# Mixing layers' weights split one layer ahead; a conv and a state space scan without GpSimd

## Chip, cores and metric

The kernel runs on one core of a Trainium2 chip. The metric is the device time of one execution in microseconds; the profile is one execution, taken by the hardware profiler. Engines: TensorE (PE; its weight loads are PEld), VectorE (DVE), ScalarE (ACT), GpSimd (POOL) and SyncE (SP), which issues every DMA.

## The reference, cut to what matters

Eight layers act on a residual stream of 512 tokens by 1024 channels: four of a first block (gated mixer a, windowed attention b, pooling mixer c, a again), then two sandwiches (mixer, feed-forward) of a second block. The change lies around the second block's mixers:

```python
def even_mixer(t, ...):                       # layer m0, the differential layer
    proj = t @ w_in
    y_a = diff_attention(proj[..., :1536])    # 4 heads, two softmaxes of width 64 each,
                                              # w = p0 - lam * p1, rmsnorm over the head
    y_b = conformer_conv(proj[..., 1536:])    # gate, causal conv of 31 taps, layernorm, silu
    return concatenate([y_a, y_b]) @ w_out

def odd_mixer(t, ...):                        # layer m1
    y_c = s5_ssm(u)       # b*u, complex scan over time with 1024 states, c*x, gelu, glu
    y_d = mla_attention(c_q, c_kv, k_r)       # 6 heads
    return concatenate([y_c, y_d]) @ w_out

def sandwich(x, g_pre, g_post, fn):
    return x + rmsnorm(fn(rmsnorm(x, g_pre)), g_post)
```

All in float32.

## The kernel before, in words

Activations lie channel by token, 128 channels to a tile of 512 tokens. A float32 product is made of three passes in fp32r: each operand is split into a high part (a copy rounded to fp32r) and a low part (the rest), and `mm3` adds high by high, high by low and low by high. For the activations `split` does it once; for the weights `wchunk` does it each time: `fetch` loads a chunk of up to 128 x 1024 into `wr`, ScalarE writes `wh`, VectorE (or GpSimd, in two halves) writes `wl = wr - wh`. Pool `pw` has three buffers of each of the three. `gemm_T` takes a chunk for one panel of 24 products, `gemm_tok` takes chunks of 24 products into four PSUM banks. After each chunk both call `tick`, which advances every generator in `tasks` by one step: that is how attention heads, the conv, the state space blocks and tables are placed among the projections. `drain` ticks until none is left. Pool `psg` has five PSUM banks for projections, head sums and turned softmaxes, `psa` three; pool `pt` has seven scratch tiles `t`.

The order in which the source issues instructions is a priority; a scheduler at build time lays out each engine's queue from it, so that work of a later step may stand earlier where an engine would be free. In `sandwich_end` TensorE and VectorE are pinned to source order.

`layer_c` (pooling, about 930 to 1285 us) runs two halves of 8 `c_wx` chunks, 8 `c_wz`, 8 half-size `c_wg` and 8 `c_wo`. `layer_m0` (from about 1643) opens with three of the eight `m0_wab` panels (conv value and gate), does the other five, then projects q and k of heads 0 and 1, all v, q and k of heads 2 and 3. `conv` does 23 of the 31 taps on VectorE (tile `cv`), eight as ScalarE products and GpSimd additions (tile `cvg`); `convs` runs the four convs, then the layer norm. Every third chunk of the q, k and v projections has its `wl` made by GpSimd (`share`). Then ticks run until all conv outputs are there, and `sandwich_end` starts with them (`k0=4`, `ahead`), projects out, adds to the residual and multiplies the first three panels of the next layer (weights `srcs`, two of them split by GpSimd). `layer_f` runs 22 gate and up panels and 24 down panels in three parts; in layer f0 the generator `ssm_tables` writes rotation tables (`srot`, `sbc`) to DRAM for m1. `layer_m1` projects, and `block` does one of eight groups of states: two fp32 products (`bu`), a rotation (`turn`: four products on VectorE, two additions on GpSimd), two scans, a rotation back, and `collect` multiplies by c on TensorE.

Of the kernel before, what the change touches and what calls it, by code (L numbers as in the profile page):

```python
# [40 lines left out]
def prepare(inp):  # L41
# [75 lines left out]
    A["m0_wo"] = _panels(np.concatenate([w[512:], w[:512]], axis=0))  # L117
# [62 lines left out]
def build(nc, tc, A, out, stages=("a0", "b", "c", "a1", "m0", "f0", "m1", "f1")):  # L180
# [40 lines left out]
    with ctx:  # L221
# [49 lines left out]
        share = [0, 0]  # L271

        def wchunk(src, n, eng=None):
# [3 lines left out]
            wr = early.pop(0) if early else fetch(src, n)  # L277
            wh = tl(pw, (P, 1024), "wh", F32R)
            wl = tl(pw, (P, 1024), "wl", F32R)
            S.activation(wh[:, :n], wr[:, :n], AF.Copy)  # L280
# [547 lines left out]
        def layer_c(nxt):  # L828
            with ExitStack() as c:
# [7 lines left out]
                for t in pads:  # L837
                    V.memset(t[:, 0:16], 0.0)
                npad = [0]
# [5 lines left out]
                for half in range(2):  # L845
                    Y = []
                    for g in (2 * half, 2 * half + 1):
# [25 lines left out]
                        for i in range(4):  # L873
                            ps = gemm_T(A["c_wg"][g, i], M)
                            V.scalar_tensor_tensor(Z[i], ps, csc[:, g * 4 + i:g * 4 + i + 1], Z[i],
                                                   op0=MUL, op1=MUL)
                            Y.append(split(py, "y", Z[i]))
                    for m in range(KD):
                        ps = gemm_T(A["c_wo"][half, m], Y)
                        V.tensor_tensor(xs[m], xs[m], ps, op=ADD)  # L880
                        if half:
                            finish_x(m)()

        def ffn_first(l):
            return [A[f"f{l}_w{n}"][i] for i in range(2) for n in "gu"] if f"f{l}" in stages else None

        def m1_first():
            return [A["m1_win"][i] for i in (2, 0, 1, 3)] if "m1" in stages else None


        def sandwich_end(W, Y, O, fresh, grow, srcs, pre=None, k0=0):
# [82 lines left out]
            if srcs:  # L974
                W1 = wchunk(srcs[1], D, G)
# [13 lines left out]
            W2 = wchunk(srcs[2], D, G)  # L989
# [55 lines left out]
        def layer_m0(nxt):  # L1045
            with ExitStack() as c:
# [3 lines left out]
                first, sc, sb = opening([A["m0_wab"][i] for i in range(3)], X)  # L1050
# [23 lines left out]
                def conv(i, up, y):  # L1074
                    def w(k):
                        return dw[:, i * 31 + k:i * 31 + k + 1]

                    def u(k):
                        return up[:, 2 + k:2 + k + NT]
                    nv = 31 - CONV_G  # L1080
                    g = tl(pm, (P, NT), "cvg")
                    for k in range(nv):
                        if k == 0:
                            V.tensor_scalar(y, u(0), w(0), cb[:, i:i + 1], op0=MUL, op1=ADD)
                            S.activation(g, u(nv), AF.Copy, scale=w(nv))
                        else:
                            V.scalar_tensor_tensor(y, u(k), w(k), y, op0=MUL, op1=ADD)
                        q = nv + 1 + k // 3
                        if k % 3 == 2 and q < 31:
                            t = tmp()  # L1090
                            S.activation(t, u(q), AF.Copy, scale=w(q))
                            G.tensor_tensor(g, g, t, op=ADD)
                        if k % 4 == 4 - 1:
                            yield
                    V.tensor_tensor(y, y, g, op=ADD)

                def convs():
# [11 lines left out]
                    ln = SumSq(4)  # L1109
# [5 lines left out]
                    rstd(r, ln.sums(), 1.0 / 512, 1e-5)  # L1115
                    lb = bcast(diagonal(r), pm, "cb")
                    yield
                    for i in range(4):
# [5 lines left out]
                        Y[i] = split(py, "y", C[i], 0.5)  # L1124
                        yield
                CV = []
                for i in range(4):
                    pu = first.pop(0) if first else gemm_T(A["m0_wab"][2 * i], X)
                    pb = first.pop(0) if first else gemm_T(A["m0_wab"][2 * i + 1], X)
# [10 lines left out]
                    if i == 0:  # L1140
                        tasks.append(convs())


                def project(a):

                    pss = gemm_tok([A["m0_wqk"][a, i] for i in range(4)], X, NT, 2)
# [27 lines left out]
                def attend(h, T):  # L1174
# [40 lines left out]
                    Y[4 + h] = split(py, "y", ps, sub)  # L1215
                share[:] = [3, 0]
                q = project(0)
                T = [flip_qk(q, 0), flip_qk(q, 1)]
                pss = gemm_tok([A["m0_wv"][i] for i in range(4)], X, NT, 2)
# [4 lines left out]
                tasks.append(attend(1, T[1]))  # L1224
                q = project(1)
# [3 lines left out]
                share[0] = 0  # L1229
                while any(Y[k] is None for k in range(4)):  # L1230
                    tick()
                sandwich_end(A["m0_wo"], Y, [tl(pa, (P, NT), "qkT") for _ in range(KD)], True, 8, ffn_first(0), k0=4)
# [134 lines left out]
        def layer_m1(nxt):  # L1367
            with ExitStack() as c:
# [34 lines left out]
                def block(j):  # L1403
# [12 lines left out]
                    def turn(a, b, minus):  # L1416

                        t1, t2, t3, t4 = tmp(), tmp(), tmp(), tmp()
                        V.tensor_tensor(t1, a, er, op=MUL)
                        V.tensor_tensor(t2, b, ei, op=MUL)  # L1420
                        G.tensor_tensor(t1, t1, t2, op=ADD if minus else SUB)  # L1421
                        V.tensor_tensor(t3, b, er, op=MUL)
                        V.tensor_tensor(t4, a, ei, op=MUL)
                        G.tensor_tensor(t3, t3, t4, op=SUB if minus else ADD)  # L1424
                        return t1, t3
                    yield
                    wr, wi = turn(bu[0], bu[1], True)
# [10 lines left out]
                    late.append((j, w, u, xr, xi))  # L1438

                def collect(j, w, u, xr, xi):  # L1440
# [3 lines left out]
                    PE.matmul(ya, lhsT=w[:, 2], rhs=xr, start=j % 4 == 0, stop=False)  # L1444
                    PE.matmul(ya, lhsT=w[:, 3], rhs=xi, start=False, stop=j % 4 == 3)
# [14 lines left out]
                def glu():  # L1460
# [4 lines left out]
                    wh, wl = wchunk(A["s_wg"], 512)  # L1465
# [27 lines left out]
                for i in range(2):  # L1493
                    ps = gemm_T(A["m1_win"][4 + i], X)
# [7 lines left out]
                wh, wl = wchunk(A["m1_wk"], 768)  # L1502
# [10 lines left out]
                wh, wl = wchunk(A["m1_wv"], 768)  # L1513
# [11 lines left out]
                for a in range(3):  # L1525
                    wh, wl = wchunk(A["m1_wq"][a], 1024)
# [53 lines left out]
                sandwich_end(A["m1_wo"], Y, O + [tl(pm, (P, NT), f"u{i}") for i in range(2)], True, 10, ffn_first(1))  # L1580


        def layer_f(l, nxt):
            with ExitStack() as c:
# [74 lines left out]
```

## Time and profile before

| | us |
|---|---|
| median of 3 runs | 2931.03 |
| lowest, highest | 2930.87, 2932.01 |
| the profiled execution | 2936.18 |
| its span, first to last instruction | 2933.7 |
| TensorE busy / VectorE / ScalarE / GpSimd | 2820.6 / 1642.2 / 1051.9 / 347.3 |
| mean granted clock of TensorE | 0.976 |

Times within the profile count from the first instruction. Matmuls are pipelined, so that a busy PE is not PE at its peak; the granted clock is 1.00 at 2.4 GHz and 0.5 at 1.2.

### The profile page before, as it was taken

The numbers are of one execution on the slowest core, as the hardware profiler recorded it, in microseconds if no ns is written. First come the engines' busy times: TensorE is split into PE (matmuls) and PEld (weight loads), VectorE is DVE, ScalarE is ACT, GpSimd is POOL, SyncE is SP. The second block draws the span as 40 slices with busy tenths as digits, with TensorE's granted clock in tenths as the row PEclk, the third lists the DMA queues.
The fourth block names the chain that finished last, engine by engine and source line by source line (L and its number), as shares of the span: only waits on it lengthen the run. The fifth ranks groups of instructions, "written<-read, shape, count | busy, mean of one in ns | idle before, by whom it ended". The sixth has DMA issues, their size and how long they took to land. (4 is left out here: it accounts for less than half of the span.)

```text
span 2933.7 us, 34524 instructions
## 1 busy us (share of the span) xinstructions
PE 2820.6 (96%) x13488; PEld 2331.9 (79%) x13488; DVE 1642.2 (56%) x3023; ACT 1051.9 (36%) x1679; POOL 347.3 (12%) x272
## 2 busy tenths in 40 slices
PE   8999999999999999999999987889999979999998
PEld 7888888888888888888888865678888845888886
DVE  4454654545556554544445697896443696543434
ACT  4322344444444322333223445442222435432222
POOL 2000000000000111210010252120000341300001
PEclk9999999999999999999999997889999999999999
DMA  4222332222223232322222211123332320132222
GB/s 161 94 86 94 129 111 87 87 80 94 72 94 95 94 101 89 120 93 94 93 94 92 90 63 44 48 96 136 111 105 92 113 90 22 58 101 100 94 99 67
DMA packets 87667, 270.08 MB, mean 92 GB/s; under 512 B 11728, under 2 KB 18640, under 8 KB 87504
## 3 DMA queue, kind: packets, MB, share of 16 engines
q1 hardware_dynamic: 87504, 267.88, 27.6%
q8 instruction: 105, 1.72, 0.2%
q14 instruction: 58, 0.48, 0.1%
HBM read 255.26 MB, written 12.58 MB: 91 GB/s over the span
## 5 line engine op out<-in xcount | busy, mean ns | idle before, releaser
L280 ACT ACTIVATE wh<-wr 128x1024 fp32r<-128x1024 f32 (+2 forms) x464 | 479.9, 1035 | 1329.8 <-PE g L205 1015.7
L205 DVE TENSOR_TENSOR wl<-wr,wh 128x1024 fp32r<-128x1024 f32 (+2 forms) x454 | 566.3, 1248 | 341.3 <-ACT wh L280 338.7
L205 PE MATMUL g<-xl,wh 128*128 128x512 f32 (+1 forms) x1720 | 661.6, 385 | 17.2 <-DVE xl L205 17.0
L205 PE MATMUL g<-xh,wh 128*128 128x512 f32 (+1 forms) x1720 | 663.7, 386 | 0.7 <-ACT wh L280 0.7
L205 PE MATMUL g<-xh,wl 128*128 128x512 f32 (+1 forms) x1720 | 658.1, 383 | 0.8 <-DVE wl L205 0.8
L205 PE MATMUL g<-wh,xh 128*128 128x512 f32 (+1 forms) x992 | 383.1, 386 | 16.9 <-ACT wh L280 8.9
L205 PE MATMUL g<-yh,wh 128*128 128x512 f32 (+1 forms) x1046 | 394.9, 378 | 1.4 <-DVE qr L205 1.4
L205 PE MATMUL g<-yh,wl 128*128 128x512 f32 (+1 forms) x1046 | 391.4, 374 | 3.1 <-DVE wl L205 3.1
L205 PEld LDWEIGHTS g<-xl,wh 128*128 128x128 f32 x1720 | 327.1, 190 | 83.0 <-DVE xl L205 22.9
L205 PE MATMUL g<-yl,wh 128*128 128x512 f32 (+1 forms) x1046 | 391.2, 374 | 0.0
L205 PE MATMUL g<-wl,xh 128*128 128x512 f32 (+1 forms) x992 | 377.8, 381 | 0.5 <-DVE wl L205 0.5
L205 PEld LDWEIGHTS g<-xh,wl 128*128 128x128 f32 x1720 | 327.3, 190 | 63.2 <-DVE wl L205 1.4
L205 PE MATMUL g<-wh,xl 128*128 128x512 f32 (+1 forms) x992 | 376.6, 380 | 0.0
L205 PEld LDWEIGHTS g<-xh,wh 128*128 128x128 f32 x1720 | 327.5, 190 | 61.2 <-ACT wh L280 1.2
L424 POOL TENSOR_TENSOR acc<-acc,t 128x256 f32<-128x256 f32 (+1 forms) x111 | 129.8, 1170 | 1654.5 <-issue 1406.4
L205 PEld LDWEIGHTS g<-wh,xh 128*128 128x128 f32 x992 | 188.5, 190 | 50.4 <-ACT wh L280 8.9
L205 PEld LDWEIGHTS g<-yh,wh 128*128 128x128 f32 x1046 | 198.4, 190 | 37.9 <-DVE qr L205 1.8
L205 PEld LDWEIGHTS g<-yh,wl 128*128 128x128 f32 x1046 | 198.1, 189 | 38.1 <-DVE wl L205 4.2
L205 PEld LDWEIGHTS g<-yl,wh 128*128 128x128 f32 x1046 | 198.3, 190 | 35.4 <-issue 1.2
L205 DVE TENSOR_TENSOR t<-g,sb 128x512 f32<-128x512 f32 x112 | 77.2, 690 | 251.4 <-PE g L205 251.4
L205 PEld LDWEIGHTS g<-wh,xl 128*128 128x128 f32 x992 | 188.4, 190 | 34.7 <-issue 0.2
L205 PEld LDWEIGHTS g<-wl,xh 128*128 128x128 f32 x992 | 188.6, 190 | 33.9 <-DVE wl L205 1.6
(315 smaller groups left out, 2728.5 us busy)
## 6 DMA issues: line engine op xcount, KB each, us to landing
wr<-in_f_wg_dram SPq DMA_DIRECT2D x44, 512.0 KB, 3.5
wr<-in_f_wu_dram SPq DMA_DIRECT2D x44, 512.0 KB, 3.5
wr<-in_a_wv_dram SPq DMA_DIRECT2D x32, 512.0 KB, 3.5
wr<-in_a_wu_dram SPq DMA_DIRECT2D x32, 512.0 KB, 3.4
wr<-in_a_wz_dram SPq DMA_DIRECT2D x32, 512.0 KB, 3.4
wr<-in_a_wo_dram SPq DMA_DIRECT2D x32, 512.0 KB, 3.5
wr<-in_b_wc_dram SPq DMA_DIRECT2D x32, 512.0 KB, 3.5
wr<-in_f_wd_dram SPq DMA_DIRECT2D x32, 512.0 KB, 3.5
```

The lines of the kernel that those rows point to most:

```text
L205: r = f(*a, **k)
L280: S.activation(wh[:, :n], wr[:, :n], AF.Copy)
L424: G.tensor_tensor(self.acc[:, t], self.acc[:, t], sq[:, t], op=ADD)
```

## The change

Weights of the two mixing layers, and the first four of the feed-forward layer behind each, are split one layer ahead: a generator `presplit` loads, splits and stores both parts to DRAM, for m0 while `layer_c` runs, for m1 while `layer_f(0)` runs. `wchunk` then loads `wh` and `wl` where it had loaded `wr` and split it. 32 weights (28 of m0, four of f0) and 24 (20 of m1, four of f1) are treated so. The differential layer's conv is all on VectorE, its sums of channels and of squares go to TensorE, two of its four conv inputs are projected later, and the rows of its output weight are reordered so that the closing projection starts with heads 0 and 1. In the state space blocks GpSimd's additions go to VectorE before the scans, and into TensorE's accumulation behind them.

```diff
 def prepare
-    A["m0_wo"] = _panels(np.concatenate([w[512:], w[:512]], axis=0))
+    A["m0_wo"] = _panels(np.concatenate([w[:256], w[512:], w[256:512]], axis=0))
...
+        def presplit(pool, todo):
+            made = []
+            def store():
+                w, wh, wl = made.pop(0)
+                nc.sync.dma_start(w.h, f32(wh))
+                nc.sync.dma_start(w.l, f32(wl))
+            for w in todo:
+                n = w.n
+                wr = tl(pool, (P, 1024), "pr")[:, :n]
+                wh, wl = (tl(pool, (P, 1024), "p" + a, F32R, bufs=2)[:, :n] for a in "hl")
+                nc.sync.dma_start(wr, w.src)
+                if made:
+                    store()
+                yield
+                S.activation(wh, wr, AF.Copy)
+                V.tensor_tensor(wl, wr, f32(wh), op=SUB)
+                made.append((w, wh, wl))
+            store()
 def wchunk
-            if eng is None:
-                share[1] += 1
-                eng = G if share[0] and share[1] % share[0] == 0 else V
+            if isinstance(src, Pre):
+                nc.sync.dma_start(f32(wh[:, :n]), src.h)
+                nc.sync.dma_start(f32(wl[:, :n]), src.l)
+                return wh, wl
...
-            step = n if eng is V else 512
-            for o in range(0, n, step):
-                e = slice(o, o + step)
-                eng.tensor_tensor(wl[:, e], wr[:, e], f32(wh[:, e]), op=SUB)
+            V.tensor_tensor(wl[:, :n], wr[:, :n], f32(wh[:, :n]), op=SUB)
 def layer_c
+                if "m0" in stages:
+                    tasks.append(presplit(newpool(c, "pre"), m0_weights() + (ffn_first(0) or [])))
...
+                    if half:
+                        drain()
                     for m in range(KD):
                         ps = gemm_T(A["c_wo"][half, m], Y)
 def sandwich_end
-                W1 = wchunk(srcs[1], D, G)
+                W1 = wchunk(srcs[1], D)
-            W2 = wchunk(srcs[2], D, G)
+            W2 = wchunk(srcs[2], D)
 def layer_m0: conv
-                    nv = 31 - CONV_G
-                    g = tl(pm, (P, NT), "cvg")
-                    for k in range(nv):
+                    for k in range(31):
...
-                            V.scalar_tensor_tensor(y, u(k), w(k), y, op0=MUL, op1=ADD)
-                        q = nv + 1 + k // 3
-                        if k % 3 == 2 and q < 31:
-                            t = tmp()
-                            S.activation(t, u(q), AF.Copy, scale=w(q))
-                            G.tensor_tensor(g, g, t, op=ADD)
-                        if k % 4 == 4 - 1:
+                            V.scalar_tensor_tensor(y, u, w, y, op0=MUL, op1=ADD)
+                        if k % 5 == 5 - 1:
                             yield
-                    V.tensor_tensor(y, y, g, op=ADD)
 convs
                     for i in range(4):
+                        while len(CV) <= i:
+                            yield
                         yield from conv(*CV[i])
-                        if i == 1:
-                            total = tl(pm, (P, NT), "cb")
-                        if i:
-                            G.tensor_tensor(total, C[0] if i == 1 else total, C[i], op=ADD)
-                    PE.matmul(ps, lhsT=ones, rhs=total, start=True, stop=True)
+                    for i in range(4):
+                        PE.matmul(ps, lhsT=ones, rhs=C[i], start=i == 0, stop=i == 3)
...
-                        ln.add(C[i], i)
+                        sq = tmp()
+                        S.activation(sq, C[i], AF.Square)
+                        sqs.append(sq)
...
+                    for n in range(4):
+                        for i in range(4):
+                            PE.matmul(ps[:, n:n + 1], lhsT=sqs[i][:, n * P:(n + 1) * P], rhs=ones[:, 0:1], ...)
 order of the layer
-                for i in range(4):                      # conv inputs
+                conv_in(0)
+                tasks.append(convs())
+                conv_in(1)
...
-                share[:] = [3, 0]
                 q = project(0)
...
                 tasks.append(attend(0, T[0]))
                 tasks.append(attend(1, T[1]))
+                conv_in(2)
                 q = project(1)
...
                 tasks.append(attend(2, T[0]))
                 tasks.append(attend(3, T[1]))
-                while any(Y[k] is None for k in range(4)):
+                conv_in(3)
+                while any(Y[k] is None for k in range(2)):
                     tick()
-                sandwich_end(A["m0_wo"], Y, ..., True, 8, ffn_first(0), k0=4)
+                sandwich_end([pre("m0_wo", m) for m in range(KD)], Y, ..., True, 8, ffn_first(0), k0=2)
 def layer_m1: block
-                    wr, wi = turn(bu[0], bu[1], True)
+                    if late:
+                        collect(*late.pop())
+                    t1, t2, t3, t4 = tmp(), tmp(), tmp(), tmp()
...
+                    V.tensor_tensor(t1, t1, t2, op=ADD)
...
+                    V.tensor_tensor(t3, t3, t4, op=SUB)
...
-                    if late:
-                        collect(*late.pop())
-                    xr, xi = turn(sr, si, False)
+                    xs_ = [(2, tmp()), (2, tmp()), (3, tmp()), (3, tmp())]
+                    V.tensor_tensor(xs_[0][1], sr, er, op=MUL)
+                    V.scalar_tensor_tensor(xs_[1][1], si, -1.0, ei, op0=MUL, op1=MUL)
+                    V.tensor_tensor(xs_[2][1], si, er, op=MUL)
+                    V.tensor_tensor(xs_[3][1], sr, ei, op=MUL)
 collect
-                    PE.matmul(ya, lhsT=w[:, 2], rhs=xr, start=j % 4 == 0, stop=False)
-                    PE.matmul(ya, lhsT=w[:, 3], rhs=xi, start=False, stop=j % 4 == 3)
+                    for n, (a, x) in enumerate(xs_):
+                        PE.matmul(ya, lhsT=w[:, a], rhs=x, start=j % 4 == 0 and n == 0, stop=j % 4 == 3 and n == 3)
 def layer_f
                         if l == 0 and i == 2 and "m1" in stages:
+                            tasks.append(presplit(newpool(c, "pre"), m1_weights() + (ffn_first(1) or [])))
                             tasks.append(ssm_tables(ptab))
```

The other calls only pass `pre(...)`, the two DRAM tiles of a weight, where they passed the weight.

## Rows read from the trace of the kernel before

**Rows 1.** The page: busy us of each engine; busy tenths and clock in 40 slices.

```profile
PE 2820.6 (96%) x13488; PEld 2331.9 (79%) x13488; DVE 1642.2 (56%) x3023; ACT 1051.9 (36%) x1679; POOL 347.3 (12%) x272
...
PE   8999999999999999999999987889999979999998
...
PEclk9999999999999999999999997889999999999999
```

**Rows 2.** Stretches: length, busy (count) of PE, PEld, DVE, ACT, POOL; clock, DMA, GB/s.

```profile
940.00:1105.00 165.00, 164.94 (x734) 136.18 (x733) 93.17 (x133) 59.45 (x78) 20.91 (x12) 1.00 0.30 99
1957.00:2095.00 138.00, 138.00 (x615) 114.02 (x614) 88.43 (x250) 41.20 (x56) 0.00 (x0) 1.00 0.37 126
1661.00:1858.00 197.00, 159.12 (x657) 120.40 (x656) 169.56 (x303) 97.12 (x197) 69.59 (x44) 0.83 0.14 49
1858.00:1957.00 99.00, 85.14 (x490) 76.22 (x490) 88.52 (x329) 38.28 (x72) 30.91 (x31) 0.89 0.23 78
2264.00:2346.00 82.00, 74.67 (x448) 66.69 (x448) 53.96 (x104) 34.08 (x62) 29.11 (x30) 0.94 0.34 111
2346.00:2431.00 85.00, 66.09 (x230) 41.99 (x229) 77.22 (x103) 28.33 (x52) 38.47 (x28) 0.88 0.27 87
2431.00:2496.00 65.00, 61.82 (x283) 37.05 (x282) 43.67 (x115) 39.97 (x93) 10.74 (x8) 1.00 0.04 13
2496.00:2577.00 81.00, 75.49 (x470) 67.84 (x468) 40.91 (x70) 35.06 (x67) 29.77 (x29) 0.96 0.22 72
```

**Rows 3.** Waits of PE, 1661 to 1858: who ended them, us, times, longest.

```profile
PE a L205 <- DVE mxc L205: 11.6, 3, 10.8
PE g L205 <- DVE t L205: 8.0, 1, 8.0
```

**Rows 4.** Groups of VectorE, 1661 to 1858: count, busy us, mean ns, idle before.

```profile
L205 DVE SCALAR_TENSOR_TENSOR cv<-up,m_dw,cv 128x512 f32<-128x512 f32 x88 | 85.8, 1020 | 0.1
L205 DVE TENSOR_TENSOR wl<-wr,wh 128x1024 fp32r<-128x1024 f32 x14 | 20.9, 1493 | 1.9 <-ACT wh L280 1.9
...
L205 DVE TENSOR_SCALAR cv<-up,m_dw,m_cb 128x512 f32<-128x512 f32 x4 | 4.1, 1029 | 0.0
...
L205 DVE TENSOR_TENSOR cv<-cv,cvg 128x512 f32<-128x512 f32 x4 | 2.7, 676 | 0.0
...
L205 DVE TENSOR_TENSOR t<-qk,m_cos 128x128 f32<-128x128 f32 x8 | 2.3, 284 | 1.5 <-ACT qk L1151 1.5
```

**Rows 5.** Tile up: count, min/median/max ns, first and last start.

```profile
L205 DVE SCALAR_TENSOR_TENSOR cv<-up,m_dw,cv x88: 733/740/1895, 1666.5 to 1783.2; 128x512 f32<-128x512 f32 x88
...
L205 DVE TENSOR_SCALAR cv<-up,m_dw,m_cb x4: 535/1030/1522, 1665.9 to 1736.3; 128x512 f32<-128x512 f32 x4
```

**Rows 6.** Stretches near the start, columns as in Rows 2.

```profile
8.00:12.00 4.00, 3.07 (x6) 1.99 (x7) 3.13 (x3) 4.00 (x7) 1.81 (x2) 1.00 1.03 408
12.00:16.00 4.00, 4.00 (x19) 3.29 (x18) 4.00 (x3) 4.00 (x8) 3.58 (x3) 1.00 1.04 370
```

**Rows 7.** Waits of SP, 940 to 1105.

```profile
SPq L254 <- DVE wl L205: 155.2, 36, 9.8
```

**Rows 8.** Groups of VectorE, 2346 to 2496.

```profile
L205 DVE TENSOR_TENSOR t<-t,E 128x512 f32<-128x512 f32 x32 | 27.6, 896 | 1.1 <-POOL t L1421 1.1
L205 DVE TENSOR_TENSOR_SCAN t<-mag,t 128x512 f32<-128x512 f32 x16 | 27.3, 1724 | 1.2 <-POOL t L1421 1.2
...
L205 DVE TENSOR_TENSOR wl<-wr,wh 128x1024 fp32r<-128x1024 f32 x6 | 8.7, 1470 | 0.0
```

**Rows 9.** Tiles mag and E: min/median/max ns of scan and product.

```profile
L205 DVE TENSOR_TENSOR_SCAN t<-mag,t x16: 1192/1589/2304, 2351.4 to 2450.1; 128x512 f32<-128x512 f32 x16
...
L205 DVE TENSOR_TENSOR t<-t,E x32: 657/678/1778, 2356.7 to 2454.7; 128x512 f32<-128x512 f32 x32
```

**Rows 10.** Groups of PE, 2346 to 2496.

```profile
L205 PE MATMUL a<-u,bc 128*128 128x512 f32 x32 | 15.4, 603 | 5.3 <-DMA bc<-sbc 5.3
```

**Rows 11.** Waits of PE, 2264 to 2346.

```profile
PE g L205 <- DVE xl L205: 5.6, 7, 1.8
```

More of the change, by code (lines that the diff above doesn't have):

```diff
@@ L882, in layer_c, with pre, m0_weights, m1_weights @@
                             finish_x(m)()
+        PRE = {}
+        def pre(name, *ix):
+            k = (name,) + ix
+            if k not in PRE:
+                a = A[name]
+                for i in ix:
+                    a = a[i]
+                PRE[k] = Pre(a, a.shape[-1])
+            return PRE[k]
         def ffn_first(l):
-            return [A[f"f{l}_w{n}"][i] for i in range(2) for n in "gu"] if f"f{l}" in stages else None
+            return [pre(f"f{l}_w{n}", i) for i in range(2) for n in "gu"] if f"f{l}" in stages else None
         def m1_first():
-            return [A["m1_win"][i] for i in (2, 0, 1, 3)] if "m1" in stages else None
+            return [pre("m1_win", i) for i in (2, 0, 1, 3)] if "m1" in stages else None
+        def m0_weights():
+            return ([pre("m0_wab", i) for i in range(8)] + [pre("m0_wqk", a, i) for a in range(2) for i in range(4)]
+                    + [pre("m0_wv", i) for i in range(4)] + [pre("m0_wo", m) for m in range(KD)])
+        def m1_weights():
+            return (m1_first() + [pre("m1_win", i) for i in (4, 5)] + [pre("m1_wk"), pre("m1_wv")]
+                    + [pre("m1_wq", a) for a in range(3)] + [pre("s_wg")] + [pre("m1_wo", m) for m in range(KD)])
         def sandwich_end(W, Y, O, fresh, grow, srcs, pre=None, k0=0):
@@ L1049, in layer_m0 @@
                 X = state["X"]
-                first, sc, sb = opening([A["m0_wab"][i] for i in range(3)], X)
+                first, sc, sb = opening([pre("m0_wab", i) for i in range(3)], X)
                 new_norm(nxt)
@@ L1108, in convs @@
                     yield
[L1109 removed]
+                    sqs = []
                     for i in range(4):
                         V.tensor_tensor(C[i], C[i], mu, op=SUB)
[L1112 removed]
+                        sq = tmp()
+                        S.activation(sq, C[i], AF.Square)
+                        sqs.append(sq)
                     yield
                     r = small(4, "lnr")
[L1115 removed]
+                    ps = psum_a()
+                    for n in range(4):
+                        for i in range(4):
+                            PE.matmul(ps[:, n:n + 1], lhsT=sqs[i][:, n * P:(n + 1) * P], rhs=ones[:, 0:1],
+                                      start=i == 0, stop=i == 3)
+                    rstd(r, ps[:, 0:4], 1.0 / 512, 1e-5)
                     lb = bcast(diagonal(r), pm, "cb")
@@ L1214, in attend @@
                         PE.transpose(ps[:, i * P:(i + 1) * P], o[:, i * P:(i + 1) * P], ident)
-                    Y[4 + h] = split(py, "y", ps, sub)
-                share[:] = [3, 0]
+                    Y[h if h < 2 else 4 + h] = split(py, "y", ps, sub)
                 q = project(0)
                 T = [flip_qk(q, 0), flip_qk(q, 1)]
-                pss = gemm_tok([A["m0_wv"][i] for i in range(4)], X, NT, 2)
+                pss = gemm_tok([pre("m0_wv", i) for i in range(4)], X, NT, 2)
                 vt = tl(pm, (P, 4, NT), "vt")
@@ L1228, in layer_m0 @@
                 tasks.append(attend(3, T[1]))
-                share[0] = 0
-                while any(Y[k] is None for k in range(4)):
+                conv_in(3)
+                while any(Y[k] is None for k in range(2)):
                     tick()
-                sandwich_end(A["m0_wo"], Y, [tl(pa, (P, NT), "qkT") for _ in range(KD)], True, 8, ffn_first(0), k0=4)
+                sandwich_end([pre("m0_wo", m) for m in range(KD)], Y, [tl(pa, (P, NT), "qkT") for _ in range(KD)], True, 8, ffn_first(0), k0=2)
         def ssm_tables(p):
@@ L1579, in layer_m1 @@
                 O = [t[:, a] for t in [tl(pm, (P, 2, NT), "E", bufs=3) for _ in range(3)] for a in range(2)]
-                sandwich_end(A["m1_wo"], Y, O + [tl(pm, (P, NT), f"u{i}") for i in range(2)], True, 10, ffn_first(1))
+                sandwich_end([pre("m1_wo", m) for m in range(KD)], Y, O + [tl(pm, (P, NT), f"u{i}") for i in range(2)], True, 10, ffn_first(1))
         def layer_f(l, nxt):
@@ L1614, in layer_f @@
                             V.tensor_tensor(O[m], O[m], ps, op=ADD)
-        pdr0 = newpool(ctx, "pdr0", space=bass.MemoryType.DRAM)
         mag = tl(pc, (P, 8), "mag")
```

58 lines of the change are left out of this document (27 added, 31 removed).

## Prediction

> **What bounds the kernel now.** I read the page first. TensorE is busy 2820.6 us of the 2933.7 us span, and in most of the 40 slices it shows 9 tenths at the full clock; the slices that show less lie around two places, and there the granted clock falls too [rows 1]. A change that leaves those two places alone could win nothing, and one that puts work into the others must not make TensorE wait there.
>
> Then the stretches [rows 2]. In dense stages 734 matmuls take 164.9 us, 0.2247 us each, so a chunk of 24 matmuls takes 5.4 us. The weak places are the differential layer, 1661 to 1858 (PE busy 159 of 197 us at clock 0.83, VectorE 170), its closing projection to 1957 (99 us, VectorE 88.5), and the state space part, 2346 to 2496 (150 us, VectorE 77.2 + 43.7). The waits of PE in the first stretch end on VectorE: 11.6 us for a softmax maximum, 8.0 us for a conv input [rows 3]. So VectorE sets the pace there, but not by its sum alone: 170 of 197.
>
> Last, what fills VectorE. In 1661 to 1858 it is 88 conv taps at a mean of 1020 ns and 14 weight splits at 1493 ns [rows 4]. The tile's own view gives taps of 733, median 740, up to 1895 ns [rows 5]: the mean is not what a tap costs but what it costs beside GpSimd's 69.6 us of work in that stretch [rows 2]. The state space scans show the same, 1192 at least and 2304 at most [rows 9], mean 1724 [rows 8].
>
> **The change part by part.** *Differential layer, TensorE's side.* After the opening, up to the end of the second head projection, come 12 + 24 + 96 + 96 + 48 + 96 = 372 matmuls, 83.6 us at 0.2247, and with some 14 us for turning q and k and for banks changing hands (an estimate) 98 us. Nothing there waits for a split any more; a chunk is two loads of 512 KB per 5.4 us, 194 GB/s, which is far under the 370 GB/s of [rows 6]. *VectorE's sum.* Removed: 14 splits, 20.9, and four additions of GpSimd's part, 2.7. The 88 taps at 85.8 become 120 at 0.74, 88.8; the four first taps go from 4.1 to 4 x 0.535 = 2.1 [rows 4, 5]. 169.6 - 20.9 - 2.7 + 3.0 - 2.0 = 147 us. TensorE's need: 159 us at clock 0.83 is 132 us at the full one; three more 512-column products with ones at about 1 us [rows 10] and eight more sums of one column add 5: 137. So the stretch could shrink to about 147, by 50 us, and no further.
>
> *What hinders that is order.* The last of the four conv inputs is projected only after the second head projection, so its 31 taps (22.7 us) come after 98 us, and so does most of the rest of VectorE's work. That rest is 169.6 - 85.8 - 20.9 - 4.1 - 2.7 = 56 us before; the conv inputs (12 instructions at 0.68) and the turning of q and k (some 32 at 0.28 or less, [rows 4]) are 15 of it, so about 41 us are heads and layer norm. 98 + 23 + 41 = 162, and the norm's chain (product with ones, squares, sums, power, spread, all through other engines) holds VectorE some 13 us more, since the four conv outputs must be there before the closing projection can go on. 175 against 197: I take **-22**, bounds -50 and 0. At 0 the five PSUM banks of psg would hold: a projection takes four, and the two heads beside it need one each for their sum and one for turning, so that the heads stand until the projection is done, as they do before.
>
> *Closing projections.* Ten splits leave VectorE and two GpSimd in each of the three that end in a next layer. PE waits there mostly for xl of the update, 5.6 us in the second [rows 11], and that chain stays. In exchange, a weight whose buffer comes free late now needs two loads after that instead of one ACT and one VectorE pass. The first one is 99 us long, the third, with VectorE at half the load, 81 [rows 2]: bound -18. I take **-5** for all three, because VectorE's load in the first is in part the next stage's tables, which remain; other end +4.
>
> *State space part.* Per block, VectorE takes two additions from GpSimd, and the two of the turn back go to TensorE as two more matmuls. Sum for VectorE: scans 27.3 to 16 x 1.19 = 19.0; products 27.6 to 32 x 0.678 = 21.7; additions 16 x 0.68 = +10.9; splits -9.6 (six of 8.7, and one of 768 columns, [rows 8, 9]). 120.9 - 8.3 - 5.9 + 10.9 - 9.6 = 108. TensorE: 16 more fp32 products of 512 columns, each two instructions; 32 such cost 15.4 us [rows 10], so +15.4, against a need now of 66 x 0.88 + 62 = 120: 135. In the first 85 us VectorE is the bound and 10 us go; in the last 65 TensorE is busy 62 us already, and three blocks' extra products land there. I take **-9**; bounds -15 (150 to 135) and +5 (only the extra products felt).
>
> *Splitting one layer ahead.* This adds work where TensorE is full. In the pooling layer 32 weights (28, and four of the feed-forward layer) are loaded, split, and stored twice: 32 x 1.573 = 50.3 MB, 32 ACT and 32 VectorE passes. VectorE there is at 93 of 165 us; 32 x 1.26 more over 156 us leave it under 85%, ACT under 60% [rows 2]. Each entry also makes SP wait: the load of the next raw weight waits for the subtraction of the last one (one buffer), and behind it on SP stand two stores and the main loop's next load. SP now waits 155 of 165 us for a buffer [rows 7]: its loads run up to three chunks, 16 us, ahead of use, and that covers a subtraction that comes some us late. If the cover is gone, each late one shows in full.
>
> The bytes are the tighter thing. One entry per chunk, 33 chunks (25 of 24 matmuls, eight of 12): 156 us, in which 50.3 + 15.2 = 65.5 MB would move, 419 GB/s. The rows give 408 and 370 in windows where the DMA share is over 1 [rows 6]: 160 or 177 us, so +4 to +21; by the busy share (99 GB/s at 0.30, so 330) 198 us, +42. Against that the single buffer makes an entry wait for its own load, and there are 53 chunks before the layer needs the queue empty: over those 243 us it is 304 GB/s, under all three. I take **+3**, range 0 to +42. The feed-forward layer: 24 entries (36 MB), 13 MB of its own and 4 MB of tables over 25 chunks, 135 us: 393 GB/s. **+2**, range 0 to +26.
>
> The Trainium skill speaks against this part: "DMA: Bandwidth & Descriptors", Specifications, gives about 358 GB/s as what a core gets from HBM, under what these stretches ask. The trace disagrees for short times (408 and 370 in 4 us windows, [rows 6]); whether it does for 150 us no row shows. By 358 the two stretches cost 65.5/358 = 183, so +27, and 148, so +13.
>
> Nothing is hidden elsewhere: the store to DRAM lies hundreds of us ahead of its load. Sum: -22 - 5 - 9 + 3 + 2 = **-31**. The profiled execution took 2936.2 us around its 2933.7 span, 5 us over the median of 2931.0 shown; taken off that median it gives **2900 us**.
>
> **The rivals.** *Heads held by banks, last conv late.* The first stretch stays near 197; what is left is -5 - 9 + 5, and a few us of it: about 2920. For it: the one bank left over, and that VectorE has 64 us of work after the second projection. Against it: the splits alone leave 20.9 us less to do.
> *All of it.* The stretch goes to 147 (-50), the closings -10, state space -15, nothing lost: 2856. For it: both sums allow it. Against it: the norm at the end.
> *Slower: the DMA engines become the bound in the pooling and feed-forward layers.* TensorE, dense now, waits for weights. At 330 GB/s, +42 and +26 against -36 is +32: 2963. It decides from where 118.5 MB take 36 us more than the 291 us of both stretches, at 362 GB/s if the entries come one per chunk.
> *Nothing gained in total.* The same mechanism at a rate near that point, 360, between the 330 by share and the 370 of the lower window: 118.5/360 = 329 us, +38 against -36, 2933. For it: only the start of the kernel shows more. Against it: the single buffer, as above. The page named above states a rate near this one.
>
> **How the numbers follow.** The forecast (2880 to 2915) has 0.55, banks and late conv 0.17, all of it 0.13, slower 0.08, nothing 0.07. 0.2%, 6 us, is about what a measurement can tell from no change. Faster: 0.55 + 0.17 + 0.13 = 0.85; within: 0.07; slower: 0.08. The range must leave out no more than 0.2: it drops the slower case and that of no change (0.15) and a little of the far end of all of it: 2862 to 2928.
>
> **What would show it.** In the changed profile: taps at a mean near 0.74 us and scans near 1.2; no split of the differential layer's weights in its stretch; the second head projection ends some 100 us after the opening and VectorE is full from there to the layer norm's end; the closing projection starts about 175 us after the opening. In the pooling layer 24 matmuls still take 5.4 us while the DMA share reaches 0.9 or more; PE waits there for wh or for a DMA would be the slower rival. Two things would make the prediction wrong: gaps of PE between 940 and 1105, or a differential layer that stays at 197 us although its splits are gone.

## The result: slower, by 0.8%

| | us | to the kernel before |
|---|---|---|
| before, median beside it | 2930.95 (2927.76 to 2932.01) | |
| after, median of 4 runs | 2952.35 (2949.98 to 2959.45) | ratio 1.0079, 95% interval 1.006 to 1.0098 |
| predicted | 2900 (2862 to 2928) | |

The page after, against [rows 1]: busy time by engine, three of the 40 slices' lines, the queue of loads and stores, and the bytes of HBM.

```profile
PE 2836.1 (96%) x13542; PEld 2329.9 (79%) x13542; DVE 1623.1 (55%) x3077; ACT 1034.0 (35%) x1647; POOL 213.2 (7%) x187
...
PE   8999999999999999999999998789999899999997
...
DMA  4222332222224788342222342258852350332232
GB/s 161 93 86 94 130 114 80 93 75 90 73 99 131 247 302 297 122 130 94 91 93 93 136 171 86 75 170 304 303 175 95 116 195 29 115 107 99 94 98 66
...
q1 hardware_dynamic: 119760, 383.24, 38.2%
...
HBM read 312.94 MB, written 70.25 MB: 130 GB/s over the span
```

Two hills stand in the DMA line that were not there: the pooling layer (slices 13 to 16) and the feed-forward layer f0 (27 to 30), up to 304 GB/s. TensorE is busy 15.5 us longer, with 54 products more, which says nothing of where the time went; that is read from the layers. Each layer's opening ends with a product with ones (tile `a<-t,ones`). The table gives the time from one such product to the next; c is the pooling layer, a1 the gated mixer behind it, m0 and m1 the mixers of the second block and f0 the feed-forward layer between them:

| us | first to c | c | a1 | m0 | f0 | m1 |
|---|---|---|---|---|---|---|
| before | 951.5 | 316.0 | 357.9 | 295.6 | 386.1 | 233.8 |
| after | 960.3 | 341.4 | 357.9 | 281.4 | 391.0 | 226.2 |
| difference | +8.8 | +25.4 | 0.0 | -14.2 | +4.9 | -7.6 |

The layers that were to gain do gain: 14.2 and 7.6 us. The pooling layer, where the splitting for m0 runs, costs 34.2 with its opening, and f0, where that for m1 runs, 4.9. (The expectations below say 34.6; they count from the span's start.)

Times scatter with the granted clock: the profiled execution of before took 2936.2 us at 0.976, where its runs near 2928 show 0.979 to 0.983, so 5 to 8 us of the gains of m0 and m1 may be that execution's own, and one run of an experiment below (3162.4 us at 0.843) is left out of its median. By the medians all gains together are 39.1 - 21.4, about 18, where m0 and m1 make 21.8 in the table. The dense layers don't move with it: in five runs without splitting for m1 f0 takes 384.8 to 385.0, and in four without any the pooling layer takes what it takes before.

The pooling layer after, by stretches of 50 or 60 us (columns: length; PE, PEld, DVE, ACT, POOL busy; clock; DMA share; GB/s), where [rows 2] had 0.30 and 99 GB/s, and what PE waited for there:

```profile
940.00:1000.00 60.00, 52.77 (x227) 42.44 (x226) 37.75 (x43) 29.03 (x36) 12.27 (x8) 0.94 0.81 274
1000.00:1050.00 50.00, 50.00 (x223) 41.39 (x222) 34.64 (x54) 22.26 (x29) 1.90 (x1) 1.00 0.68 235
1050.00:1100.00 50.00, 45.51 (x190) 36.08 (x189) 32.00 (x46) 21.74 (x28) 4.82 (x3) 0.95 0.87 297
1100.00:1150.00 50.00, 48.58 (x207) 38.81 (x206) 24.55 (x25) 15.67 (x16) 0.00 (x0) 0.98 0.88 303
1150.00:1200.00 50.00, 42.25 (x163) 31.70 (x162) 29.68 (x41) 17.42 (x21) 10.95 (x8) 0.93 0.76 261
1200.00:1250.00 50.00, 50.00 (x222) 41.27 (x221) 26.63 (x41) 13.14 (x17) 17.12 (x12) 1.00 0.27 90
```

```profile
PE g L205 <- ACT wh L309: 8.6, 9, 2.4
PE a L205 <- DVE t L205: 5.9, 1, 5.9
PE g L205 <- DVE wl L205: 5.9, 8, 1.2
```

A dense 50 us holds 222 matmuls; here they are 223, then 190, 207 and 163, until the entries end near 1180 and 222 are back. PE waits for the main loop's own splits, `wh` and `wl`, and those for loads that went out late and landed late; once, in the opening, it waits for VectorE's `t`. The loads of `c_wx`, before and after (count, size, median us from issue to landing):

```profile
wr<-in_c_wx_dram SPq DMA_DIRECT2D x16, 512.0 KB, 3.4
```

```profile
wr<-in_c_wx_dram SPq DMA_DIRECT2D x16, 512.0 KB, 6.0
```

Waiting is not all of it. In the six stretches PE stands idle for 20.9 of 310 us, and the clock column, 0.93 to 0.98 in the four stretches with waits, stands for 20.4 us at 1.2 instead of 2.4 GHz, in four pieces; before, the clock is 1.00 throughout this layer. At half speed that is some 10 us more (an estimate), so that about a third of the 34.2 is paid in clock.

SP's timeline shows how the loads come to be late (start, length, line, transfer):

```profile
1099.94 0.33 SPq L286 DMA_DIRECT2D preh<-ph  x1
1101.20 0.33 SPq L292 DMA_DIRECT2D pr<-in_m_wo_dram  x1
1101.58 0.45 SPq L287 DMA_DIRECT2D prel<-pl  x1
1102.08 0.42 SPq L254 DMA_DIRECT2D wr<-in_c_wo_dram  x1
1106.72 0.33 SPq L286 DMA_DIRECT2D preh<-ph  x1
1107.98 0.33 SPq L292 DMA_DIRECT2D pr<-in_m_wo_dram  x1
1108.37 0.44 SPq L287 DMA_DIRECT2D prel<-pl  x1
1108.86 0.42 SPq L254 DMA_DIRECT2D wr<-in_c_wo_dram  x1
1113.60 0.33 SPq L286 DMA_DIRECT2D preh<-ph  x1
```

It is a ring: `pr` goes out at 1101.20, lands 4.5 us later, ScalarE's copy (1.03) lets `preh` go at 1106.72, VectorE's subtraction (1.25) lets the next `pr` go at 1107.98. One turn takes 6.8 us here, and in most turns one load of the main loop passes, where TensorE uses one in 5.4. The 32 entries ran from 936.8 to 1179.7, 7.17 us apart in the median; 40 loads of the main loop went out in that time (eight of them half-size), where before 51 did (twelve half-size).

The differential layer after, VectorE, between the opening and the closing projection (name, count, busy, mean ns, idle before it), beside [rows 4, 5], and the scans of the state space part beside [rows 8, 9]:

```profile
L205 DVE SCALAR_TENSOR_TENSOR cv<-up,m_dw,cv 128x512 f32<-128x512 f32 x120 | 87.1, 751 | 1.4
L205 DVE CUSTOM_DVE_ANT_0 P<-a,cmask 128x384 f32<-128x384 f32 (+1 forms) x16 | 9.8, 620 | 10.2 <-PE a L205 9.2 <-ACT P L1078 1.0
...
L205 DVE TENSOR_TENSOR t<-g,sb 128x512 f32<-128x512 f32 x4 | 2.8, 690 | 7.2 <-PE g L205 5.9 <-ACT sb L507 1.2
```

```profile
L205 DVE TENSOR_TENSOR_SCAN t<-mag,t 128x512 f32<-128x512 f32 x16 | 19.4, 1219 | 0.4
```

Taps and scans take what their tile's rows promised (751 and 1219 ns), but VectorE now stands idle in front of the scores and the last conv input: it waits for TensorE, and is busy 140 of the 189 us.

### The profile page after: what moved, and what is told of

It reads as the page before. It is cut to its first block, busy times and chain, and to the rows that moved or that the text cites. A ratio compares the mean times of both kernels' runs of the same rounds, so it can differ in the third digit from the quotient of the medians.

```text
span 2950.1 us, 34873 instructions
## 1 busy us (share of the span) xinstructions
PE 2836.1 (96%) x13542; PEld 2329.9 (79%) x13542; DVE 1623.1 (55%) x3077; ACT 1034.0 (35%) x1647; POOL 213.2 (7%) x187
## 5 line engine op out<-in xcount | busy, mean ns | idle before, releaser
L309 ACT ACTIVATE wh<-wr 128x1024 fp32r<-128x1024 f32 (+2 forms) x408 | 420.8, 1033 | 1027.6 <-PE g L205 786.5
L205 DVE TENSOR_TENSOR wl<-wr,wh 128x1024 fp32r<-128x1024 f32 (+2 forms) x408 | 508.8, 1248 | 308.6 <-ACT wh L309 305.6
L205 PE MATMUL g<-yh,wh 128*128 128x512 f32 (+1 forms) x1046 | 398.5, 381 | 11.4 <-ACT yh L421 4.8
L450 POOL TENSOR_TENSOR acc<-acc,t 128x256 f32<-128x256 f32 (+1 forms) x109 | 121.3, 1113 | 1708.7 <-issue 1412.9
```

What stands on the lines that cost most here:

```text
L205: r = f(*a, **k)
L450: G.tensor_tensor(self.acc[:, t], self.acc[:, t], sq[:, t], op=ADD)
```

## The experiments

Two theories of the loss. *Queue*: SP stands in the ring above, and the main loop's loads behind it. *Bytes*: the DMA engines are full with loads and stores together. Costs below are of the pooling layer with its opening (first to c, and c), against before.

**No splitting ahead, the rest as changed.**

```diff
-                if "m0" in stages:
-                    tasks.append(presplit(...))       # layer_c
-                            tasks.append(presplit(...))   # layer_f(0)
-                PRE[k] = Pre(a, a.shape[-1])
+                PRE[k] = a
```

> All of the change but the splitting ahead: no weight goes through DRAM, every chunk is loaded raw and split where it is used, on VectorE alone. If the 34.6 us by which the pooling layer with its opening grew and the 4.9 us of the feed-forward layer come from the splitting ahead, both go back (pooling layer 316 us from opening to opening, feed-forward 386), and m0 gives back part of its 14 us, since 28 splits of 1.25 us return to VectorE there: 2915 us, 2905 to 2930. Rival: the pooling layer is slow for another reason (its queue laid out differently): it stays over 335 us and the total near 2950.

2910.6 us against 2927.5, ratio 0.9942 (0.9927 to 0.9957): faster than before, by 0.6%. c takes 316.0 again, f0 384.9, m0 278.4 and m1 226.7. So the whole loss is the splitting ahead, and it gained next to nothing in return: m0 is 3 us shorter with its splits back on VectorE and ScalarE, m1 half a us longer.

**A second raw buffer**, paid for with one of the two high buffers.

```diff
-                wr = tl(pool, (P, 1024), "pr")[:, :n]
-                wh, wl = (... bufs=2 ...)
+                wr = tl(pool, (P, 1024), "pr", bufs=2)[:, :n]
+                wh, wl = (... bufs=1 for "h", 2 for "l")
```

> The splitting ahead with two buffers for the raw weight and one for the high part, so that a raw load need not wait for the subtraction of the one before; bytes unchanged. Theory A (one entry's cycle of landing 4.6, ScalarE 1.06, VectorE 1.25 us holds SP's queue, and the main loop's load goes out once per cycle of 7 us): the cycle gets shorter, the pooling layer loses 12 to 25 of its 34.6 us, total near 2935. Theory B (the 16 DMA engines are full at about 300 GB/s): nothing changes beyond 4 us.

2942.7, 1.0053 (1.0036 to 1.007); cost 24.2, a saving of 10.0, between the two theories. Entries lie 6.1 us apart, and the DMA engines are fuller. The transfers of 1040 to 1140, first in the changed kernel, then here:

```profile
DMA packets 8447, 29.77 MB, mean 298 GB/s; under 512 B 935, under 2 KB 935, under 8 KB 8443
...
q1 hardware_dynamic: 8443, 29.71, 86.6%
```

```profile
DMA packets 9217, 32.56 MB, mean 326 GB/s; under 512 B 1023, under 2 KB 1023, under 8 KB 9213
...
q1 hardware_dynamic: 9213, 32.50, 89.5%
```

**The entries' transfers issued by GpSimd**, so that SP keeps only the main loop's.

```diff
-                nc.sync.dma_start(w.h, f32(wh))      # and w.l, and wr
+                G.dma_start(w.h, f32(wh))
```

> The loads and stores of the splitting ahead are issued by GpSimd instead of SP; bytes unchanged, the main loop's loads no longer stand behind a wait for ScalarE or VectorE. Theory A (queue): the pooling layer loses 20 us or more of its 34.6, total near 2928. Theory B (bytes): it stays within 8 us of the changed kernel's 341 us.

3005.4, 1.0268 (1.0253 to 1.0284); cost 52.2, and f0 424.7, more than either theory had expected (c alone takes 356.2). SP then waits for hardly anything but its own buffers, yet all is slower: from 1050 to 1250 the DMA engines move 242 GB/s at a share of 0.71 and PE is busy 180.5 of 200; the clock is at its lower level for 37.5 us of the layer. So taking SP out of the ring is no cure, and a shared queue alone does not make the cost. The Trainium skill ("DMA: Bandwidth & Descriptors", Issuing engine by pattern) calls the path from SyncE generally the faster one; this run agrees in its sign: the entries' loads land 4.95 us after issue in the median, against 4.55. Why the kernel is this much slower stays open.

**Two ticks to an entry.**

```diff
                 if made:
                     store()
                 yield
+                yield
```

> One entry of the splitting ahead for every two chunks instead of one. Both theories: while it lasts, half the bytes per time and half the blocked queue, so TensorE waits vanish there; 26 of the 32 entries fit before the pooling layer empties the list, the other six fall into its last chunks. Theory A and B: the pooling layer's 34.6 us go to 10 or less, total near 2928. Rival: the emptying of the list costs 7 us for each of six entries, the layer stays at +30 or more.

2942.3, 1.0051 (1.0036 to 1.0066); cost 22.9, where both theories had expected 10 or less. The pace in time fell less than in ticks: entries lie 7.7 us apart, against 7.17, presumably since the build's scheduler lays them out by readiness. The engines move as much as in the changed kernel while the entries last (274 GB/s against 276), but 46 main loads stand between them instead of 40: at one rate the cost differs by 11 us, presumably by the order on the queue.

**Stores of 64 columns**, every instruction of the ring kept.

```diff
+                if not full: (the first pair is stored whole, and read by all)
+                else:
-                nc.sync.dma_start(w.h, f32(wh))
+                    nc.sync.dma_start(w.h[:, :64], f32(wh)[:, :64])   # and w.l
```

> The changed kernel with every instruction and wait of the splitting ahead kept, but after the first entry each store writes 64 columns instead of all of them, and the mixing layers load every weight from the one pair that was stored whole (so those layers multiply by the wrong weights). The pooling layer then moves some 16.8 MB of raw weights beside its own, and 2 to 3 MB of stores instead of 33.5. Theory 'bytes': the loss in the pooling layer is the rate at which the DMA engines move loads and stores together; the pooling layer with its opening costs at most 10 us over the kernel before (34.6 in the changed one) and the whole comes to 2915 to 2928. Theory 'queue': the loss is SP standing behind each entry's waits and the extra instructions of ScalarE and VectorE; 24 us or more of the cost remain and the whole is 2940 or more. In between, the shares divide by the number.

2927.5, 0.9989 (0.9978 to 1.0); cost 10.0. Entries lie 6.0 us apart, as with the second raw buffer, at less than half its cost; whole main loads land 4.3 us after issue here and 5.5 there. The stretches are dense again but for one, at a share of 0.54 to 0.58 instead of 0.68 to 0.88:

```profile
1000.00:1050.00 50.00, 50.00 (x222) 41.40 (x222) 35.30 (x52) 23.97 (x30) 3.85 (x2) 1.00 0.57 182
1050.00:1100.00 50.00, 45.14 (x193) 35.47 (x192) 33.23 (x44) 22.39 (x29) 3.81 (x2) 1.00 0.54 173
1100.00:1150.00 50.00, 50.00 (x223) 41.41 (x222) 27.52 (x31) 17.87 (x18) 2.99 (x2) 1.00 0.58 189
```

**Loads in place of the stores**, same size, same place in the queue.

```diff
-                    nc.sync.dma_start(w.h[:, :64], f32(wh)[:, :64])
+                    nc.sync.dma_start(f32(wh), w.src)                 # and wl
```

> As the run with small stores, but each entry's two stores are two loads of the same size: the raw weight is loaded again into the entry's own split buffers, at the same place of SP's queue and behind the same instructions (the mixing layers again multiply by the one pair stored at the start, so by the wrong weights). The pooling layer then moves the same 50.3 MB beside its own as the changed kernel, all of it loads. Theory 'total bytes': what the DMA engines move in all is the limit, whatever the direction; the pooling layer with its opening costs 28 us or more over the kernel before (34.6 with stores, 10.0 with small ones), the whole 2945 or more. Theory 'stores are dearer': loads move at the 370 to 408 GB/s seen at the kernel's start, 65.5 MB of them in 160 to 177 us; the cost is 12 to 22 us and the whole 2929 to 2940.

2931.5, 1.0004 (0.9993 to 1.0016); cost 24.2, between the two theories. In the same 100 us (1040 to 1140):

```profile
DMA packets 8824, 31.15 MB, mean 311 GB/s; under 512 B 979, under 2 KB 979, under 8 KB 8818
...
q1 hardware_dynamic: 8818, 31.06, 85.1%
```

So of 34.2 us about 10 stay when hardly a byte is stored, 14 come from moving 33.5 MB more, and 10 from their being stores. The order on SP is laid out anew at each build and is not quite the same in the three, so the shares are rough. About half of the last 10 is clock (an estimate): TensorE idles 20.9 us more than before with stores and 16.0 with loads, and its clock is at the lower level for 20.4 and 10.2 us. f0 took 391.7 with small stores and 384.1 with loads: its 5 us go with the stores, large or small, and what in them is not settled.

**The conv's taps back on GpSimd**, and **GpSimd's splits back**, both without splitting ahead.

```diff
+ conv() of the kernel before                                     # first kernel
+ every third wl of q, k and v in two halves on GpSimd            # second kernel
```

> The changed kernel without splitting ahead, with the conv's taps as in the kernel before: 23 of 31 on VectorE, eight as ScalarE products and GpSimd additions; the order of the projections and the sums on TensorE stay as changed. If GpSimd's taps are what slowed VectorE (taps at 1020 ns instead of 750) and so the layer, the differential layer goes back from 278 to about 290 us and the whole to about 2922. If its gain comes from the order and from the norm's sums, it stays within 3 us of 278.

> The changed kernel without splitting ahead, with every third weight of the differential layer's head projections split by GpSimd in two halves, as in the kernel before. If GpSimd's splits slow VectorE or arrive late, the differential layer takes 282 to 290 us instead of 278; if VectorE's sum were the bound, taking four splits off it would gain up to 5 us.

2912.6, 0.9937 (0.9917 to 0.9957), m0 280.3; and 2916.2, 0.9951 (0.9933 to 0.9969), m0 284.2. Against 278.4, the taps are worth 1.9 us and the splits 5.8. VectorE's taps take 922 ns in the mean with GpSimd's part back, 753 without.

**All four conv inputs first**, without splitting ahead.

```diff
-                conv_in(1)
+                for i in range(1, 4):
+                    conv_in(i)
...
-                conv_in(2)
-                conv_in(3)
-                    up = tl(pm, (P, 32 + NT), f"up{i % 2}")
+                    up = tl(pm, (P, 32 + NT), f"up{i % 3}")
```

> The changed kernel without splitting ahead, with all four conv inputs projected before q and k as in the kernel before (three buffers for the conv's padded input instead of two, so that the third input does not wait for the first conv). Theory 'late conv': the differential layer is 278 us opening to opening because VectorE must do the fourth conv's 31 taps and the layer norm after the second head projection; with the inputs early VectorE works through the projections and the layer falls to 255 to 268 us, the whole to about 2893. Rival 'chain of the heads': what TensorE waits for at the end is scores, softmax, turn and sum of the heads, one after another, so that earlier taps only push the heads' VectorE work back: 275 us or more, the whole 2907 or more.

2895.6 (median of three runs), 0.9881 (0.9856 to 0.9906): the lowest of all. m0 takes 261.4. VectorE (third number) is full until the projections end at 1761, and no longer idle beside them:

```profile
1700.00:1720.00 20.00, 20.00 (x96) 15.83 (x95) 20.00 (x42) 8.23 (x16) 0.00 (x0) 1.00 0.23 80
1720.00:1740.00 20.00, 20.00 (x90) 16.58 (x89) 20.00 (x28) 6.81 (x8) 0.00 (x0) 1.00 0.30 105
1740.00:1760.00 20.00, 19.91 (x92) 15.14 (x91) 19.16 (x46) 7.67 (x20) 0.00 (x0) 1.00 0.16 53
```

**The same order with splitting ahead**, and **with it for 12 weights alone** (q, k and v of m0, three ticks to an entry).

```diff
-                PRE[k] = a
+                PRE[k] = Pre(a, a.shape[-1]) if name in ("m0_wqk", "m0_wv") else a    # second kernel
```

> The changed kernel, splitting ahead included, with all four conv inputs projected before q and k (three padded input buffers). Without splitting ahead that order gives a differential layer of 261 us, and VectorE is busy 20 of 20 us there until the projections end, 17 us of it with 14 splits. Theory 'VectorE is the bound once the convs are early': with the splits gone the layer falls to 244 to 252 us. Rival 'the heads' chain is the bound': it stays at 259 us or more, as taking the splits away gained nothing in the changed order. The pooling and feed-forward layers lose about 35 and 5 us in either case, so the whole is 2916 to 2924 or 2931 and more.

> All conv inputs early, and of the splitting ahead only the 12 weights that the differential layer's q, k and v projections use, three ticks per entry, in the pooling layer (18.9 MB over it instead of 50.3, all m1 weights raw). Without any splitting ahead this order takes about 2897 us. If VectorE is the bound in the layer, it falls from 261 to 246 to 254 us; the pooling layer pays by share of the entries (12 of 32 of 34.6 us) 13 us if the entries run close together, 4 to 6 if the pace spreads them: 2885 to 2905 in all. If the heads' chain is the bound, nothing is gained and the whole is 2902 to 2910.

2939.1, 1.002 (1.0009 to 1.0031), m0 265.7; and 2900.6, 0.9894 (0.9874 to 0.9914), m0 254.8 at a cost of 7.7. For twelve weights the splits are worth 6.6 us in m0 and cost 7.7 in the pooling layer, which is about even (the two intervals overlap); with all split ahead m0 is longer than with none, 265.7 against 261.4.

When PE has the conv's first output and goes on with the closing projection (before: starts it), counted from m0's opening, and the rest of m0 behind that:

| us | closing goes on at | from there to f0's opening |
|---|---|---|
| before | 196.6 | 99.0 |
| after | 188.9 | 92.5 |
| no splitting ahead | 190.8 | 87.6 |
| conv inputs first, none ahead | 173.7 | 87.7 |
| conv inputs first, all ahead | 173.2 | 92.5 |
| conv inputs first, twelve ahead | 167.1 | 87.7 |

With the inputs first the taps no longer hold the closing. With all split ahead the last tap ends 101.7 us after the opening, with none 149.0, yet the sums of the conv outputs on TensorE begin at 147.0 and 148.2 and the closing goes on at 173.2 and 173.7. So taking splits off a full VectorE moved the taps by 47 us and the end by half a us. Whether the heads' chain holds those sums or their place in TensorE's order, and why twelve ahead gain what all ahead don't, no run separates.

## Why the prediction was wrong, by its steps

**Splitting one layer ahead: the step that failed.** Forecast +3 and +2, measured +34.2 and +4.9. With this term as measured and the rest as forecast the sum is -36 + 39.1, +3 instead of -31; the other 18 us to the measured +21 are gains that came out smaller, the first stretch of m0 above all. The step is the choice of +3 out of 0 to +42: "there are 53 chunks before the layer needs the queue empty: over those 243 us it is 304 GB/s, under all three". I took a slow entry for a harmless one, because its bytes then stay under the limits. The entries did take 243 us (936.8 to 1179.7), but that is luck: in this time 40 loads of the main loop went out, not 53, and 276 GB/s were moved, not 304. Eight of the 40 are half-size, so they are 36 whole chunks, 194 us of TensorE's work, and 49 us are missing; the 16 us of loads ahead that I counted as cover leave 33 (an estimate), and 34.2 was measured. The cover was used up once, not once per entry.

Why main loads were that few and that late is shown in part. The ring's pace is not enough: at 6.1 and 6.0 us to an entry the second raw buffer costs 24.2 and the small stores 10.0, and with the entries on another queue the cost rises to 52.2. Most of it, about 24, goes when the stores' bytes go, although at 276 GB/s in the mean these bytes stay under every limit that I had compared them with.

**The slower rival** (2963, "TensorE, dense now, waits for weights") has the right place and sign, and its sign in the profile, PE waiting for `wh` at a DMA share near 0.9, is there. Its mechanism is half of it: small stores leave 10.0 of the 34.2, a second raw buffer 24.2. Bytes and ring work on each other: `pr` lands 4.5 us after issue in the changed kernel, 3.6 with small stores, at a share of 0.56 instead of 0.81 while the entries last. What full engines would move can be estimated from the rate and share of 100 us: 326/0.895 = 364 and 311/0.851 = 365 GB/s, and 298/0.866 = 344 in the changed kernel. The Trainium skill ("DMA: Bandwidth & Descriptors", Specifications) says about 358; by these estimates the trace agrees, though none of these runs moved more than 326 over the 100 us. The 408 of [rows 6] does not last that long.

**First stretch of m0: -22 forecast, -7.7 measured** (196.6 to 188.9). The forecast had the late fourth conv in it, at 98 + 23 + 41 + 13 us. What it left out: that conv's own 48 matmuls come after the second head projection (which ends at 94), so that the projections end at 118.8, the last tap at 168.0, and the norm's chain takes 21 us to 188.9, not 13. With the inputs first the projections end at 98.9 and the closing goes on at 173.7. That is the rival "last conv late", shown for these 17 us; the banks, left alone, did not hold them (the third padded buffer is part of the edit). The 20.9 us of removed splits were no reason: back on VectorE they move the closing by 1.9 us, and VectorE has room for them, busy 140 of 189 us without and 160 of 191 with them. [rows 2 to 4] gave VectorE's sum, 170 of 197; a sum under the span doesn't say that the engine sets the pace.

**Closing projections: -5 for three forecast.** The first gained 6.5. The other two show little: without splitting ahead f0 is 1.2 us shorter than before, and m1's gain is there by its last scan. Two things are in the first one: without splitting ahead it gains 11.4, and with it 4.9 of that is lost again, in either order of the conv inputs. What PE waits for there, after, and without splitting ahead:

```profile
PE a L205 <- DVE t L205: 5.6, 1, 5.6
PE g L205 <- DVE xl L205: 4.9, 7, 1.1
PE g L205 <- ACT yh L421: 4.8, 1, 4.8
PE g L205 <- DMA wh<-preh: 3.4, 1, 3.4
```

```profile
PE g L205 <- DVE xl L205: 5.8, 9, 0.9
PE g L205 <- ACT yh L421: 4.8, 1, 4.8
PE g L205 <- DVE wl L205: 3.6, 2, 3.4
PE a L205 <- DVE t L205: 2.3, 1, 2.3
```

The wait for `wh<-preh` is the one that I named ("needs two loads after that instead of one ACT and one VectorE pass") and priced within the -5; it takes the place of one for `wl`, 3.6. Most of the rest is a later sum of squares, 5.6 against 2.3. Whether the 11.4 are GpSimd's two splits there or the rows' new order wasn't separated.

**State space part: right.** -9 forecast; the last scan ends 8.2 us earlier after the opening (108.2 to 100.0), and m1 is 7.6 shorter, 7.1 without splitting ahead, so the splitting has next to no part in it. How much of it the profile of before adds (its clock is at the lower level for 20.5 us there, after's for 6.8) is open. The scans fell from a mean of 1724 ns to 1219, as [rows 9] let expect.

## What to carry to other kernels

A mean rate under a limit does not make work free in a queue that also feeds the bound engine: ask how many of that engine's loads get through while the work lasts, and how late they land, and count a lead of some chunks once. A run that keeps every instruction and cuts the bytes tells two prices apart; here it took 24 of 34.2 us away. Before taking work off an engine, see whether it idles in that stretch and for whom; here moving two inputs of a long serial piece forward was worth 17 us, and taking 14 splits away from the same stretch 2. When a change has parts in different layers, time from opening to opening names the part at fault in one table.

## What the runs showed that was not expected

- Stores cost more than loads of the same size at nearly the same place: 34.2 us against 24.2 for 33.5 MB, some 5 of the difference by the clock, and f0's 5 us vanish with loads.
- The waits of TensorE came with clock: in the pooling layer, at 2.4 GHz throughout before, it runs at 1.2 GHz for 20.4 us.
- One core's transfers would fill up near 344 to 365 GB/s over 100 us (estimates from rate and share); a load of 512 KB that lands in 3.4 us otherwise takes 6.0 then.
- Issued by GpSimd the same transfers made the kernel 53 us slower than issued by SyncE (3005.4 against 2952.4).
- VectorE's taps at 753 instead of 922 ns, with GpSimd out of the way, were worth 1.9 us of the layer; VectorE had room there.
